# The order of the second half's turning and of its sums, and the last row tile's scaling, in a one-core decoder layer

## The chip, the cores and the metric

The kernel runs on one core of a Trainium2 chip. The metric is the device time of one execution in microseconds (us); of the kernel before there are three runs.

## What is computed

One decoder layer on x (1024 rows by 1024 channels): a layer norm, one input projection of the result h to 11,296 columns, two mixers on its parts (a gated short convolution and a chunked state-space scan), their output projections, a merge, a last projection and a layer norm of the residual. Cut to what matters here:

```
h = layer_norm(x, ln_in_g, ln_in_b)
proj = h @ w_in[i]
u, b_gate, c_gate, z_a, z_s, xbc, dt_raw, g_a, g_s = jnp.split(proj, offsets, axis=-1)
...
out = mixed @ w_o[i]
h = layer_norm(DEEPNORM_ALPHA * h + out, ln_g[i], ln_b[i])
```

## The kernel before

The input projection takes its weights' column tiles in 44 pairs of 128 + 128 columns. Each pair is multiplied with h by the seven products of a fast (Strassen-Winograd) 2x2 scheme. On the weights' side a pair has the blocks a11, a12, a21, a22 and four sums made of them: s1 = a21 + a22, s2 = s1 - a11, s3 = a11 - a21 (`combine`, L232) and s4 = a12 - s2 (`combine_last`, L248). On the side of h the four quarters (b11 and b21 from rows 0 to 511, b12 and b22 from rows 512 to 1023, each 512 of the 1024 channels) give four sums t1 = b12 - b11, t2 = b22 - t1, t3 = b22 - b12 and t4 = b21 - t2 (`quarter_sums`). Product 1 uses b11, 2 b21, 3 s4 with b22, 4 t4, 5 s1 with t1, 6 s2 with t2, 7 s3 with t3.

Every operand is split in two: a high part, a copy in TensorE's single-pass float32 format, and a low part, the remainder (`sub_split`, L104, shown as L105). A product of 128x128 weights with 512 columns is then three matmuls: high x high, high x low, low x high. The four k tiles of 128 channels make 12 matmuls for one product of one pair. The high part of a weight block is named whi, its low part wlo; there are four buffers of the one and three of the other. ACT makes the high parts of weights (L288; L286 for the chained ones of the first three pairs), DVE the low ones. The bank of a product is named p with product and pair (p3_0), or pU for products 1, 6 and 7. A t or b tile of one k with both its parts is a unit (`unit`).

The first three pairs run product by product, in the order 1, 2, 3, 6, 5, 7, 4 (pair 0, 1, 2 in each), since the quarters of the second half come later. Before, once products 1 and 2 are made, `dt_project(0)` makes a projection of 32 columns (the bank dps, copied by ACT to dT; a second half of it, `dt_project(1)`, and the transposes of dT follow among the matmuls of product 5), and `second_half` (L441) turns the rows 512 to 1023 by transposes on TensorE into eight banks, k = 4 to 7 (giving b22) and then 0 to 3 (giving b12). ACT scales each bank into hf (L394) and, for b22, DVE makes the unit: a cast (L398) and a remainder (L105). Product 3 needs b22, products 6, 5, 7 and 4 the sums.

The order on each engine comes from a scheduler that places instructions when their operands are expected, except where the code chains them: `q(engine, ...)` puts an instruction behind the last one that went through `q` on that engine. From the fourth pair on, `pin` keeps every engine in the order in which the code is written. Within an engine instructions run in their order. Before, the sums for the weights of the first three pairs are made on POOL through `q`, the first of the late ones held back until the layer norm's last scaling on DVE (`normed`); the operations of `quarter_sums` are left to the scheduler, k by k.

At the end the rows go out in eight tiles. `norm_out` (L1162) takes the mean and variance of a tile, ACT scales it (L1176), POOL multiplies and adds (L1177, L1178), SP sends it. For the last tile DVE does the first 832 columns alone (L1172, L1173) and ACT's queue sends those; the other 192 go the usual way.

## Time and profile before

| | |
|---|---|
| median of three runs (lowest, highest) | 1408.17 us (1406.65, 1409.61) |
| the profiled execution's own time | 1411.06 us |
| span from its first to its last instruction | 1408.9 us |
| mean granted TensorE clock | 0.992 |
| busy: PE, DVE, ACT, POOL | 1378.9, 975.2, 701.7, 485.3 us |

The engines are PE (TensorE), DVE (VectorE), ACT (ScalarE) and POOL (GpSimd); SP only issues transfers. A row of the order of time gives the start, the duration of one or of a merged run (xN), the engine, the line of the kernel's code, the operation, the output and inputs by tile name, and in brackets the idle time ahead of it and what ended that. Buffer numbers are left out of names, so `t<-t` stands for a t unit made from one of the sums. The granted clock is TensorE's clock as a share of its full one. PE's matmuls overlap: each row lasts 0.39 us, where the next starts earlier.

### The profile page before, as it was taken

The page shows a single profiled execution, that of the slowest core. Times are in us where ns is not written, and L with a number is a line of the kernel's source. Part 1 is how long each engine was busy: PE and PEld are TensorE (multiplying, and loading weights), DVE is VectorE, ACT ScalarE, POOL GpSimd, SP SyncE. Part 2 cuts the span into 40 slices and gives each one's busy share as a digit, 9 for nine tenths or more (in the row PEclk, how much of TensorE's full clock was granted, in tenths as well). Part 3 has the DMA queues.
Part 4 walks back from the last instruction along what each step waited for, and adds up shares of the span by engine and source line. Part 5 has one row for each costly group of instructions (what it writes and reads, how often), then busy time and mean ns, then how long its engine had stood idle before and what let it go on. Part 6 is the DMA issues. An engine that isn't in the chain of part 4 may idle for free.

```text
span 1408.9 us, 18441 instructions
## 1 busy us (share of the span) xinstructions
PE 1378.9 (98%) x6532; PEld 1110.0 (79%) x6532; DVE 975.2 (69%) x1422; ACT 701.7 (50%) x1228; POOL 485.3 (34%) x367
## 2 busy tenths in 40 slices
PE   8799999999999999999999999999999999999997
PEld 5577887888888888888888888888878888888886
DVE  8867779787779878688878686867464463224766
ACT  4565565656567555566566565555452231113431
POOL 1312215453435444334444343444230000000487
PEclk9899999999999999999999999999999999999999
DMA  6022363564454555544555445543457763223422
GB/s 239 16 76 94 115 145 110 129 180 129 141 134 133 153 155 147 131 131 130 151 157 187 132 154 127 153 128 127 172 174 269 232 222 139 100 75 110 144 90 90
DMA packets 166459, 198.09 MB, mean 141 GB/s; under 512 B 10688, under 2 KB 116064, under 8 KB 166368
## 3 DMA queue, kind: packets, MB, share of 16 engines
q1 hardware_dynamic: 158160, 167.14, 40.9%
q10 hardware_dynamic: 8208, 29.79, 5.3%
q8 instruction: 51, 0.84, 0.2%
q14 instruction: 40, 0.33, 0.1%
HBM read 146.28 MB, written 50.61 MB: 140 GB/s over the span
## 4 chain that ended last, share of the span: by engine, by line
PE 91%; DVE 4%; issue 2%; ACT 1%; POOL 1%; DMA 0%; ACTq 0%; POOLq 0%; DVEq 0%
PE p L1020 11%; PE p L1021 11%; PE p L1022 11%; PE pU L1020 8%; PE pU L1022 8%; PE pU L1021 8%; PE p_ws L859 4%; PE p_ws L860 4%; PE p_ws L861 4%; PE ya L691 2%; PE st L696 2%; PE p_wa L859 2%; PE p_wa L860 2%; PE p_wa L861 2%; PE p_wo L1157 2%
## 5 line engine op out<-in xcount | busy, mean ns | idle before, releaser
L105 DVE TENSOR_TENSOR wlop<-raw_a,whip 128x512 fp32r<-128x512 f32 x210 | 185.0, 881 | 160.5 <-ACT whip L288 64.7
L1020 PE MATMUL p<-b,whip 128*128 128x512 f32 x352 | 143.8, 409 | 7.6 <-ACT whip L286 4.8
L1020 PE MATMUL pU<-t,whip 128*128 128x512 f32 x352 | 145.2, 414 | 0.0
L1020 PE MATMUL p<-t,whip 128*128 128x512 f32 x352 | 142.0, 403 | 0.0
L1021 PE MATMUL p<-b,whip 128*128 128x512 f32 x352 | 140.4, 399 | 0.0
L1022 PE MATMUL p<-b,wlop 128*128 128x512 f32 x352 | 139.8, 398 | 0.0
L1021 PE MATMUL pU<-t,whip 128*128 128x512 f32 x352 | 139.3, 396 | 0.0
L1022 PE MATMUL p<-t,wlop 128*128 128x512 f32 x352 | 139.1, 395 | 0.0
L1021 PE MATMUL p<-t,whip 128*128 128x512 f32 x352 | 139.1, 395 | 0.0
L1022 PE MATMUL pU<-t,wlop 128*128 128x512 f32 x352 | 139.0, 395 | 0.0
L676 POOL TENSOR_TENSOR xw<-xd,dte_t 128x256 f32<-128x256 f32 x56 | 46.9, 837 | 260.5 <-DVE xd L662 260.5
L288 ACT ACTIVATE whip<-raw_a 128x512 fp32r<-128x512 f32 x207 | 125.8, 622 | 19.2 <-issue 10.5
L942 POOL TENSOR_TENSOR res<-res,ag 128x1024 f32<-128x1024 f32 x8 | 19.7, 2464 | 276.1 <-ACT res L941 276.1
L239 POOL TENSOR_TENSOR s<-raw_a,raw_a 128x512 f32<-128x512 f32 x42 | 69.6, 1657 | 92.1 <-DVE wlop L105 87.8
L860 PE MATMUL p_ws<-y,whis 128*128 128x512 f32 x256 | 100.9, 394 | 0.0
L859 PE MATMUL p_ws<-y,whis 128*128 128x512 f32 x256 | 100.8, 394 | 0.0
L861 PE MATMUL p_ws<-y,wlos 128*128 128x512 f32 x256 | 100.7, 393 | 0.0
L105 DVE TENSOR_TENSOR wlos<-raw_s,whis 128x512 fp32r<-128x512 f32 x32 | 22.1, 692 | 113.0 <-PE p_ws L861 89.2
L253 POOL TENSOR_TENSOR raw_a<-raw_a,s 128x512 f32<-128x512 f32 x42 | 67.5, 1606 | 90.2 <-issue 78.7
L105 DVE TENSOR_TENSOR wlop<-s,whip 128x512 fp32r<-128x512 f32 x84 | 80.2, 966 | 13.2 <-PE p L1022 8.5
L1020 PEld LDWEIGHTS p<-b,whip 128*128 128x128 f32 x352 | 67.0, 190 | 23.7 <-ACT whip L286 5.1
L288 ACT ACTIVATE whis<-raw_s 128x512 fp32r<-128x512 f32 x32 | 20.3, 634 | 129.6 <-PE p_ws L860 109.0
(225 smaller groups left out, 3404.7 us busy)
## 6 DMA issues: line engine op xcount, KB each, us to landing
raw_a<-in_w_in_dram SPq DMA_DIRECT2D x168, 256.0 KB, 4.0
em<-cum_d SPq DMA_DIRECT2D x64, 256.0 KB, 6.8
xg_d<-cv ACTq DMA_DIRECT2D x16, 512.0 KB, 7.0
xT<-xg_d SPq DMA_DIRECT2D x32, 256.0 KB, 4.7
z<-zs_d SPq DMA_DIRECT2D x32, 256.0 KB, 3.1
gat_d<-y SPq DMA_DIRECT2D x32, 256.0 KB, 2.8
gt<-gat_d SPq DMA_DIRECT2D x16, 512.0 KB, 6.4
raw_s<-in_w_s_dram SPq DMA_DIRECT2D x32, 256.0 KB, 4.3
```

The costliest lines, as they stand in the source:

```text
L105: return eng.tensor_tensor(lo, full, hi.bitcast(F32), ALU.subtract)
L239: fs = [lambda: Gp.tensor_tensor(s1, r["a21"], r["a22"], ALU.add), lambda: Gp.tensor_tensor(s2, s1, r["a11"], ALU.subtract), lambda: Gp.te ...
L253: f = lambda: Gp.tensor_tensor(a12, a12, s1s[p]["s2"], ALU.subtract)
L288: S.activation(flat(hi), src, AF.Copy)
L676: Gp.tensor_tensor(xw, XD[n, i], dte_t[:, hs, c].unsqueeze(2).to_broadcast([P, HG, HD]), ALU.mult)
L691: PE.matmul(YA[n][o:o + HD, t * P:(t + 1) * P], lhsT=XD[n, i][:, h, :], rhs=EM[n, i][:, h, :], start=True, stop=True)
L859: PE.matmul(ps, lhsT=hi[:, k, :], rhs=u[:, 0, :], start=start, stop=False)
L860: PE.matmul(ps, lhsT=hi[:, k, :], rhs=u[:, 1, :], start=False, stop=False)
L861: PE.matmul(ps, lhsT=lo[:, k, :], rhs=u[:, 0, :], start=False, stop=stop)
L1020: PE.matmul(ps, lhsT=hi[:, k, :], rhs=u[:, 0, :], start=first, stop=False, skip_group_check=True)
L1021: PE.matmul(ps, lhsT=hi[:, k, :], rhs=u[:, 1, :], start=False, stop=False, skip_group_check=True)
L1022: PE.matmul(ps, lhsT=lo[:, k, :], rhs=u[:, 0, :], start=False, stop=(k == 3), skip_group_check=True)
```

## The change

`second_half` becomes two parts. `lower_quarter` turns the banks k = 4 to 7 right after products 1 and 2, all 16 transposes, through `q`, ahead of the four evacuations. `upper_quarter` turns k = 0 to 3 after product 3 of pair 0. The sums of pair 1, and the last sum of pair 0, move from POOL to DVE. Pair 2's sums stay on POOL and wait until DVE has made the last b22 unit (`b22_done`). `quarter_sums` now makes all four tiles of t2, then t1, t3 and t4, with its sums, copies and remainders chained by `q`, some of them in place of b11. The units lie in other buffers (`PLACE`). The matmuls of products 3 and 6 of the first three pairs are chained as well. In `norm_out` ACT's scaling stands ahead of DVE's two operations and of the transfer on its queue, and DVE takes 704 columns of the last tile, ACT and POOL 320.

```diff
     B = {}
-    PLACE = {"t2": 0, "t1": 1, "t3": 2, "t4": 3}
+    PLACE = {"t2": range(4), "t1": range(4, 8), "t3": range(9, 16, 2), "t4": range(8, 16, 2)}
     def b_unit(n, k):
-        i = 4 * k + PLACE[n] if n in PLACE else 16 + 4 * ("b11", "b21", "b22").index(n) + k
+        i = PLACE[n][k] if n in PLACE else 16 + 4 * ("b11", "b21", "b22").index(n) + k
         B[n, k] = unit(i, f"{n}_{k}")
         return B[n, k]
...
         r = raws["p", p]
         s1, s2 = (est.tile([P, HALF], F32, name=f"e{n}_{p}") if p < 2 and n == "s1" else
                   r["a11"] if p < 2 else ap.tile([P, HALF], F32, tag=n, name=f"{n}_{p}") for n in ("s1", "s2"))
-        fs = [lambda: Gp.tensor_tensor(s1, r["a21"], r["a22"], ALU.add),
-              lambda: Gp.tensor_tensor(s2, s1, r["a11"], ALU.subtract),
-              lambda: Gp.tensor_tensor(r["a21"], r["a11"], r["a21"], ALU.subtract)]
+        eng = V if p == 1 else Gp
+        fs = [lambda: eng.tensor_tensor(s1, r["a21"], r["a22"], ALU.add),
+              lambda: eng.tensor_tensor(s2, s1, r["a11"], ALU.subtract),
+              lambda: eng.tensor_tensor(r["a21"], r["a11"], r["a21"], ALU.subtract)]
         if p < 2:
             fs = [fs[0], fs[2], fs[1]]
-        for f in fs:
-            q(Gp, f) if p < EARLY else f()
+        for i, f in enumerate(fs):
+            ins = q(eng, f) if p < EARLY else f()
+            if p == 2 and i == 0:
+                tc.add_manual_dep(ins.ins, b22_done[0].name,
+                                  mybir.DependencyInfo(mybir.DependencyClass.Sync, mybir.DependencyReason.DATA), reason="later")
         s1s[p] = {"s1": s1, "s3": r["a21"], "s2": s2}
     def combine_last(p):
...
         if "s4" in s1s[p]:
             return
         a12 = raws["p", p]["a12"]
-        f = lambda: Gp.tensor_tensor(a12, a12, s1s[p]["s2"], ALU.subtract)
-        if p < EARLY:
-            ins = q(Gp, f)
-            if p == 0:
-                tc.add_manual_dep(ins.ins, normed[0].name,
-                                  mybir.DependencyInfo(mybir.DependencyClass.Sync, mybir.DependencyReason.DATA), reason="later")
-        else:
-            f()
+        eng = V if p < 2 else Gp
+        f = lambda: eng.tensor_tensor(a12, a12, s1s[p]["s2"], ALU.subtract)
+        q(eng, f) if p < EARLY else f()
         s1s[p]["s4"] = a12
     def source(n):
...
     stats(7, 1)
     factors(6)
     norm(7, V)
-    normed = [last[V].ins]
     norm(6, S)
-    def second_half():
-        order = (4, 5, 6, 7, 0, 1, 2, 3)
-        trs = {k: bank(("c4", "tr", "st")[i % 3], f"tr1{k}") for i, k in enumerate(order)}
-        for k in order:
+    b22_done = []
+    def second_half(ks, tags):
+        trs = {k: bank(t, f"tr1{k}") for k, t in zip(ks, tags)}
+        for k in ks:
             for s in (4, 5, 7, 6):
-                PE.transpose(trs[k][:, s % 4 * P:(s % 4 + 1) * P], xs[s][:, k * P:(k + 1) * P], ident)
+                q(PE, lambda: PE.transpose(trs[k][:, s % 4 * P:(s % 4 + 1) * P], xs[s][:, k * P:(k + 1) * P], ident))
+        for k in ks:
             evac(1, k, trs[k])
-            if k in (5, 7, 1):
-                prep_hi(2 * EARLY + (5, 7, 1).index(k))
+    def lower_quarter():
+        combine_last(0)
+        prep_hi(2 * EARLY)
+        combine(1)
+        q(V, lambda: prep_lo(2 * EARLY))
+        second_half((4, 5, 6, 7), ("c4", "tr", "st", "cx"))
+        b22_done.append(last[V].ins)
+        combine_last(1)
+        prep_hi(2 * EARLY + 1)
+        q(V, lambda: prep_lo(2 * EARLY + 1))
+    def upper_quarter():
+        second_half((0, 1, 2, 3), ("cx", "st", "cx", "st"))
+        prep_hi(2 * EARLY + 2)
     def quarter_sums():
+        b11, b21, b12, b22 = ([hf[i][k][:, j * HALF:(j + 1) * HALF] for k in range(4)] for i in range(2) for j in range(2))
+        tt = [cv(f"t2_{i}") for i in range(2)]
+        t2 = [tt[k // 2][:, k % 2 * HALF:(k % 2 + 1) * HALF] for k in range(4)]
+        def split(n, k, src):
+            u = b_unit(n, k)
+            q(S, lambda: S.activation(u[:, 0, :], src, AF.Copy))
+            q(V, lambda: sub_split(u[:, 1, :], src, u[:, 0, :], V))
         for k in range(4):
-            b11, b21 = hf[0][k][:, :HALF], hf[0][k][:, HALF:]
-            b12, b22 = hf[1][k][:, :HALF], hf[1][k][:, HALF:]
-            tt = cv(f"t12_{k}"), cv(f"t34_{k}")
-            t = {"t1": tt[0][:, :HALF], "t2": tt[0][:, HALF:], "t3": tt[1][:, :HALF], "t4": tt[1][:, HALF:]}
-            V.tensor_tensor(t["t1"], b12, b11, ALU.subtract)
-            V.tensor_tensor(t["t2"], b22, t["t1"], ALU.subtract)
-            V.tensor_tensor(t["t3"], b22, b12, ALU.subtract)
-            V.tensor_tensor(t["t4"], b21, t["t2"], ALU.subtract)
-            for n in ("t2", "t1", "t3", "t4"):
-                u = b_unit(n, k)
-                S.activation(u[:, 0, :], t[n], AF.Copy)
-                sub_split(u[:, 1, :], t[n], u[:, 0, :], V)
+            q(V, lambda: V.tensor_tensor(b11[k], b12[k], b11[k], ALU.subtract))
+            q(V, lambda: V.tensor_tensor(t2[k], b22[k], b11[k], ALU.subtract))
+            split("t2", k, t2[k])
+        for k in range(4):
+            split("t1", k, b11[k])
+        for k in range(4):
+            q(V, lambda: V.tensor_tensor(b11[k], b22[k], b12[k], ALU.subtract))
+            split("t3", k, b11[k])
+        for k in range(4):
+            q(V, lambda: V.tensor_tensor(t2[k], b21[k], t2[k], ALU.subtract))
+            split("t4", k, t2[k])
...
         for k in range(4):
             first = k == 0 and (early and j in (1, 2, 3, 4, 5) or j in (1, 2, 5, 4))
             u = B[bn, k]
-            PE.matmul(ps, lhsT=hi[:, k, :], rhs=u[:, 0, :], start=first, stop=False, skip_group_check=True)
-            PE.matmul(ps, lhsT=hi[:, k, :], rhs=u[:, 1, :], start=False, stop=False, skip_group_check=True)
-            PE.matmul(ps, lhsT=lo[:, k, :], rhs=u[:, 0, :], start=False, stop=(k == 3), skip_group_check=True)
+            for w, v, stop in ((hi, 0, False), (hi, 1, False), (lo, 0, k == 3)):
+                f = lambda: PE.matmul(ps, lhsT=w[:, k, :], rhs=u[:, v, :], start=first and w is hi and v == 0, stop=stop,
+                                      skip_group_check=True)
+                q(PE, f) if 2 * EARLY <= now[0] < 3 * EARLY else f()
         oa, ob = O[p]
         oal, oah = oa[:, :HALF], oa[:, HALF:]
         if ob is not None:
...
         if n >= START and n - 2 in first_of:
             combine_last(first_of[n - 2])
         if n < START:
-            for k in range(n, min(n + LA + 1, 2 * EARLY if n < 2 * EARLY else START + LA)):
+            for k in range(n, min(n + LA + 1, 2 * EARLY if n < 2 * EARLY else 2 * EARLY + 2 if n == 2 * EARLY else START + LA)):
                 prep_hi(k)
                 if k < n + LA:
                     prep_lo(k)
...
             item_p(i, j, hi, lo)
             if n == 2 * EARLY - 1:
                 dt_project(0)
-                second_half()
+                lower_quarter()
+            if n == 2 * EARLY:
+                upper_quarter()
             if n == 3 * EARLY - 1:
                 quarter_sums()
             if n == 4 * EARLY + 1:
...
         r = res[s]
         mv = cst.tile([P, 2], F32, tag="mv", name=f"mv{s}", bufs=2)
         rs, nb = (cst.tile([P, 1], F32, tag="w" + n_, name=f"{n_}{s}", bufs=2) for n_ in ("rs", "nb"))
-        finish_stats(cst, st[s][:, :n, :], mv, rs, nb, "lo")
-        cut = 832 if last_row else 0
+        cut = 704 if last_row else 0
+        sl = slice(cut, D)
+        V.bn_aggr(mv, st[s][:, :n, :])
+        rsqrt(cst, rs, mv[:, 1:2], 1, "lo")
+        V.scalar_tensor_tensor(nb, mv[:, 0:1], -1.0, rs, ALU.mult, ALU.mult)
+        S.activation(r[:, sl], r[:, sl], AF.Identity, bias=nb, scale=rs)
         if last_row:
             V.scalar_tensor_tensor(r[:, :cut], r[:, :cut], mv[:, 0:1], lg[:, :cut], ALU.subtract, ALU.mult)
             V.scalar_tensor_tensor(r[:, :cut], r[:, :cut], rs, lb[:, :cut], ALU.mult, ALU.add)
             S.dma_start(out[s * P:(s + 1) * P, :cut], r[:, :cut])
-        sl = slice(cut, D)
-        S.activation(r[:, sl], r[:, sl], AF.Identity, bias=nb, scale=rs)
         Gp.tensor_tensor(r[:, sl], r[:, sl], lg[:, sl], ALU.mult)
         Gp.tensor_tensor(r[:, sl], r[:, sl], lb[:, sl], ALU.add)
         SP.dma_start(out[s * P:(s + 1) * P, sl], r[:, sl])
```

What the built programs hold at three places follows; numbers of tiles are kept where the set has to be seen (t3_2 is quarter k = 2 of t3, whip0_5 the high part of pair 0's weights for product 5).

On DVE, behind the last scaling of the layer norm, stood the first units of b22:

```order
L383 TENSOR_SCALAR x7_174<-x7_174,rs_t_119,nb_t_120 128x1024
L398 CAST b22_0_499<-hf10_497 128x512
L105 TENSOR_TENSOR b22_0_499<-hf10_497,b22_0_499 128x512
L398 CAST b22_1_508<-hf11_506 128x512
L105 TENSOR_TENSOR wlop0_3_567<-e0_a12_161,whip0_3_512 128x512
```

and now

```order
L376 TENSOR_SCALAR x7_174<-x7_174,rs_t_119,nb_t_120 128x1024
L252 TENSOR_TENSOR e0_a12_161<-e0_a12_161,e0_a11_150 128x512
L234 TENSOR_TENSOR es1_1_488<-e1_a21_176,e1_a22_178 128x512
L236 TENSOR_TENSOR e1_a21_176<-e1_a11_157,e1_a21_176 128x512
L235 TENSOR_TENSOR e1_a11_157<-es1_1_488,e1_a11_157 128x512
L99 TENSOR_TENSOR wlop0_3_492<-e0_a12_161,whip0_3_486 128x512
L391 CAST b22_0_516<-hf10_514 128x512
```

Four sums that POOL made, and a weight remainder, have come ahead of the first cast of b22.

On ACT, the copies that make the high parts, around the weights of product 5 (whip0_5); before:

```order
L463 ACTIVATE t2_1_649<-t12_1_643 128x512
L1045 ACTIVATE oa2_409<-p3_2_611 128x512
L463 ACTIVATE t3_1_655<-t34_1_644 128x512
L463 ACTIVATE t4_1_658<-t34_1_644 128x512
L286 ACTIVATE whip0_5_699<-es1_0_246 128x512
L463 ACTIVATE t1_2_670<-t12_2_661 128x512
L463 ACTIVATE t3_2_673<-t34_2_662 128x512
```

and now

```order
L468 ACTIVATE t3_3_672<-hf03_301 128x512
L468 ACTIVATE t4_0_676<-t2_0_625 128x512
L468 ACTIVATE t4_1_680<-t2_0_625 128x512
L468 ACTIVATE t4_2_684<-t2_1_626 128x512
L468 ACTIVATE t4_3_688<-t2_1_626 128x512
L279 ACTIVATE whip0_5_693<-es1_0_246 128x512
L279 ACTIVATE whip1_5_710<-es1_1_488 128x512
```

The copy of product 5's weights stood between the second and third quarter's copies; now it follows the last copy of t4.

On DVE, the sums and remainders of the t units; before, in the third quarter:

```order
L457 TENSOR_TENSOR t12_2_661<-hf12_518,hf02_296 128x512
L459 TENSOR_TENSOR t34_2_662<-hf12_518 128x512
L458 TENSOR_TENSOR t12_2_661<-hf12_518,t12_2_661 128x512
L105 TENSOR_TENSOR t1_2_670<-t12_2_661,t1_2_670 128x512
L460 TENSOR_TENSOR t34_2_662<-hf02_296,t12_2_661 128x512
L105 TENSOR_TENSOR t2_2_667<-t12_2_661,t2_2_667 128x512
L105 TENSOR_TENSOR t3_2_673<-t34_2_662,t3_2_673 128x512
L105 TENSOR_TENSOR t4_2_676<-t34_2_662,t4_2_676 128x512
```

and now, in the last quarter of t3 and in t4:

```order
L478 TENSOR_TENSOR hf03_301<-hf13_529 128x512
L99 TENSOR_TENSOR t3_3_672<-hf03_301,t3_3_672 128x512
L481 TENSOR_TENSOR t2_0_625<-hf00_286,t2_0_625 128x512
L99 TENSOR_TENSOR t4_0_676<-t2_0_625,t4_0_676 128x512
L481 TENSOR_TENSOR t2_0_625<-hf01_291,t2_0_625 128x512
L99 TENSOR_TENSOR t4_1_680<-t2_0_625,t4_1_680 128x512
L481 TENSOR_TENSOR t2_1_626<-hf02_296,t2_1_626 128x512
L99 TENSOR_TENSOR t4_2_684<-t2_1_626,t4_2_684 128x512
L481 TENSOR_TENSOR t2_1_626<-hf03_301,t2_1_626 128x512
L99 TENSOR_TENSOR t4_3_688<-t2_1_626,t4_3_688 128x512
L99 TENSOR_TENSOR wlop0_5_708<-es1_0_246,whip0_5_693 128x512
```

Sums of several sets stood between a sum and its remainder; now each remainder follows its own sum, and product 5's weight remainder follows all of them.

6 lines of the change are left out of this document (1 added, 5 removed).

## The prediction

> **What bounds the kernel now.** I read the page's engine table first, then what PE waited for in the first 180 us, then the granted clock in stretches of 2 us, and last the order of time on each engine. (In a row of PE waits: total us, times, longest; in a row of stretches: PE's busy us, its matmuls, the granted clock.)
>
> ```profile
> PE 1378.9 (98%) x6532; PEld 1110.0 (79%) x6532; DVE 975.2 (69%) x1422; ACT 701.7 (50%) x1228; POOL 485.3 (34%) x367
> ...
> PE p L1020 <- ACT whip L286: 4.8, 1, 4.8
> PE tr L446 <- ACT hf L394: 2.9, 3, 1.7
> ...
> PE dps L476 <- DVE t L105: 0.6, 1, 0.6
> ...
> 20.00:22.00 2.00, 1.57 (x4) 0.57 1.05 386
> 22.00:24.00 2.00, 2.00 (x7) 0.57 0.95 315
> ...
> 50.00:52.00 2.00, 0.29 (x3) 0.75 0.00 0
> ...
> 56.00:58.00 2.00, 2.00 (x6) 0.50 0.00 0
> ...
> 60.00:62.00 2.00, 2.00 (x8) 0.69 0.00 0
> 62.00:64.00 2.00, 2.00 (x10) 1.00 0.00 0
> ```
>
> PE is busy 98% of the span, so only a stretch in which it is idle or slowed can give or take time. The change touches one: the turning of the second half and the products behind it. There PE waits 4.8 us for the high part of weights, 2.9 us for banks and twice 0.6 us for t units, and then runs at clock 0.50. Now that stretch on PE:
>
> ```profile
> 42.07 0.39 PE L476 MATMUL dps<-b,wdt 128*64 128x512 f32 x1
> ...
> 55.12 0.80 PE L1020 MATMUL p<-b,whip 128*128 128x512 f32 x1 [4.82 <-ACT whip L286]
> ...
> 69.89 0.40 PE L1021 MATMUL p<-t,whip 128*128 128x512 f32 x1
> ...
> 81.38 0.39 PE L1022 MATMUL p<-t,wlop 128*128 128x512 f32 x1
> ...
> 86.51 0.40 PE L476 MATMUL dps<-b,wdt 128*64 128x512 f32 x1
> ...
> 91.65 0.40 PE L1020 MATMUL pU<-t,whip 128*128 128x512 f32 x1
> ```
>
> Product 3 starts at 55.12. The first two matmuls of product 5 of pair 0 are done by 69.89; the third, at 81.38, starts the rest of product 5, among it five dps matmuls from 86.51. At 91.65 product 7 begins. So 81.38 to 91.65, 10.27 us, held 34 matmuls of product 5, five of dps and the turning of dT, without a wait. From there on every engine's listed order is the same before and after the change until the last row tile. PE has no idle time left to absorb a shift, so I cost the first part as the shift of 91.65.
>
> **The front of the stage: what it removes.** The other engines there:
>
> ```profile
> 22.42 0.42 DVE L398 CAST b<-hf 128x512 fp32r<-128x512 f32 x1
> ...
> 23.48 0.42 DVE L398 CAST b<-hf 128x512 fp32r<-128x512 f32 x1
> ...
> 40.36 0.81 DVE L383 TENSOR_SCALAR x<-x,rs_t,nb_t 128x1024 f32<-128x1024 f32 x1
> 44.70 0.75 DVE L398 CAST b<-hf 128x512 fp32r<-128x512 f32 x1 [3.53 <-ACT hf L394]
> 45.48 1.65 DVE L105 TENSOR_TENSOR b<-hf,b 128x512 fp32r<-128x512 f32 x1
> ...
> 55.81 0.68 DVE L105 TENSOR_TENSOR b<-hf,b 128x512 fp32r<-128x512 f32 x1
> ...
> 62.07 1.89 DVE L105 TENSOR_TENSOR t<-t,t 128x512 fp32r<-128x512 f32 x3
> ...
> 41.30 1.29 POOL L253 TENSOR_TENSOR e_a<-e_a,e_a 128x512 f32<-128x512 f32 x1 [21.48 <-issue]
> ...
> 52.96 1.44 POOL L253 TENSOR_TENSOR raw_a<-raw_a,s 128x512 f32<-128x512 f32 x1
> ...
> 42.55 0.59 ACT L477 ACTIVATE dT<-dps 64x512 f32<-64x512 f32 x1 [0.95 <-PE dps L476]
> ```
>
> Three remainders in 1.89 us: a DVE operation with two SBUF inputs takes 0.60 us when they follow each other, and a split (cast and remainder) 1.06 us (22.42 to 23.48). While POOL works through its nine sums (41.30 to 54.40), the same remainder takes 1.65 us: DVE and POOL take turns, one POOL sum (about 1.1) before each DVE operation. So the split of b22 ended only at 56.49. In the changed kernel DVE makes pair 0's last sum and pair 1's three, 4 x 0.60, and a weight remainder in 41.2 to 44.4. That lies inside the 3.53 us in which DVE waited for its first bank, so it costs nothing; without that cover it would be 3.0 us. PE must now take bank c4 first and waits for the copy of dT (42.55 + 0.59), 0.7 us. The four splits then run from 44.75 to 49.0 instead of 56.49, and product 3 of pair 0 from about 45.7, paced by them. Nearly all of the old 4.8 + 2.9 us goes, and with it the slow clock of 55 to 61 us. If that were all, the change would be worth some 10 us.
>
> **Where the gain goes.** What PE needs next, the weights' high part for product 5, no longer stands among the copies of the t units on ACT but behind all of them:
>
> ```profile
> 68.13 0.63 ACT L286 ACTIVATE whip<-es 128x512 fp32r<-128x512 f32 x1
> ...
> 75.32 0.68 DVE L458 TENSOR_TENSOR t<-hf,t 128x512 f32<-128x512 f32 x1
> ...
> 76.04 0.63 ACT L463 ACTIVATE t<-t 128x512 fp32r<-128x512 f32 x1 [0.52 <-DVE t L458]
> ```
>
> At 68.13 stands the old copy, made while half of the t units were missing. In the changed order it follows the copy of t4's last quarter, which follows t4's last sum on DVE. And there each sum is followed at once by the remainder that needs ACT's copy of it: sum 0.68, 0.04 to the copy, copy 0.63, 0.03 back is 1.38 us from the sum's start (75.32 to 76.67), then the remainder 0.60, so 1.98 us a quarter where the work is 1.20. Before, other quarters' operations stood in these gaps.
>
> DVE's queue, added up from these rows: at 49.0 the splits are done. Pair 1's last sum, and a wait: PE ends product 3 of pair 0 0.5 after the last split, ACT copies its bank (0.6) and then pair 1's weights (0.63): 50.9 with the steps between. POOL's four sums of pair 2 now start at 49.0, so three DVE operations take 1.65 each: 55.9. POOL is done at 55.2; copy 0.63, three weight remainders and t2's first remainder: 59.0. t2's other quarters, two sums that hang together, copy, remainder, 2.6 each: 66.9. t1's remainders, 4 x 0.60: 69.3. t3: a first quarter of 2.4 with two bank additions in its gap, then 3 x 1.98: 77.6. t4: 3 x 1.98 gives 83.6, the last sum 0.72, its copy and the weights' copy 0.53 + 0.63: 85.5. I add 0.5 for steps between dependent operations and take **86.0**. PE has by then long done products 3 and 6 and dps, eight matmuls of which come after t1's last remainder (69.3): about 72.4. So it waits some 14 us in one piece, before product 5 of pair 0. Bounds of the 86.0: 80.5 if the gaps of t3 and t4 (7 x 0.78) were hidden, 88 if every turn with POOL and every round trip takes 0.2 more.
>
> From 86.0: 36 matmuls instead of 34 and no dps, three matmuls fewer at 10.27/39, about 0.25 each: 9.5 us at full clock. PE comes out of such a wait at half clock. By the stretches, 0.69 over 60:62 is half clock for 1.2 us of it, so the wait before 55.12 cost 6.1 us at half clock; 0.57 twice, over 20:24, is 3.4 us after a smaller wait. Half the clock loses half of that, 3.0 or 1.7 us. The wait ahead is longer than either, and I take 2.5. Product 7 then begins at 86.0 + 9.5 + 2.5 = 98.0, against 91.65: **+6.35 us**.
>
> The Trainium skill, "TensorE: Matmul & The Clock Gate", section "What's actually happening", lets one busy window of about 3.4 us end the slow state. This trace has it once as that and once nearly twice as long; by the rule alone the loss would be 1.7, an estimate, and the sum 0.8 lower.
>
> **The last row tile.**
>
> ```profile
> 1383.01 2.25 DVE L102 SCALAR_TENSOR_TENSOR nb<-mv,rs 128x1 f32<-128x1 f32 x1
> ...
> 1396.36 2.40 POOL L1177 TENSOR_TENSOR res<-res,lg 128x1024 f32<-128x1024 f32 x1 [1.43 <-ACT res L1176]
> ...
> 1401.59 0.16 DVE L102 SCALAR_TENSOR_TENSOR nb<-mv,rs 128x1 f32<-128x1 f32 x1
> ...
> 1402.77 1.08 DVE L1173 SCALAR_TENSOR_TENSOR res<-res,rs,lb 128x832 f32<-128x832 f32 x1
> ...
> 1395.04 1.24 ACT L1176 ACTIVATE res<-res,nb,rs 128x1024 f32<-128x1024 f32 x1 [4.85 <-DVE nb L102]
> ...
> 1403.95 0.37 ACTq L1174 DMA_DIRECT2D out_dram<-res  x1
> 1404.36 0.55 ACT L1176 ACTIVATE res<-res,nb,rs 128x192 f32<-128x192 f32 x1 [3.46 <-DVE res L1173]
> 1404.99 0.59 POOL L1177 TENSOR_TENSOR res<-res,lg 128x192 f32<-128x192 f32 x1 [3.79 <-ACT res L1176]
> 1405.65 0.59 POOL L1178 TENSOR_TENSOR res<-res,lb 128x192 f32<-128x192 f32 x1
> ...
> out_dram<-res ACTq DMA_DIRECT2D x1, 416.0 KB, 2.4
> out_dram<-res SPq DMA_DIRECT2D x1, 96.0 KB, 1.7
> ```
>
> Today ACT's scaling stands behind the output transfer that waits for DVE, and POOL ends at 1406.24. In the changed order ACT starts at 1401.8: 320 columns by the slope from 192 (0.55) to 1024 (1.24) are 0.66, so 1402.5. POOL takes 0.87 for 320 columns by its two rows, twice. DVE's two operations shrink to 704/832 of 1.08 = 0.92. They now run beside POOL, and a DVE operation of that form beside POOL took 2.25 instead of 0.16, so again turns: 1402.6 DVE, 1403.4 POOL, 1404.3 DVE, 1405.1 POOL. That is 1.1 us earlier, with a transfer of 160 KB, between 1.7 and 2.4, say 1.85: -0.95 us. Without turns -1.9; at worst, with both transfers meeting, -0.5.
>
> **Sum.** +6.35 - 0.95 = +5.4. The profiled execution took 1411.06 (span 1408.9 and 2.2 around it), 2.9 above the median of the runs; its own time would become 1416.5, and the median 1408.17 + 5.4 = **1413.6**. By the bounds (86.0 by -1 to +1.5 from the additions, clock 1.7 to 3.0, tail -1.9 to -0.5) this case spans 1410.8 to 1416.0.
>
> **Rivals.** About 0.2%, 2.8 us, is what the measurement of this kernel tells from no change.
>
> *The round trips are hidden* (0.11). If DVE does not stand still between a sum and its remainder in t3 and t4, the weights come at 80.5: 80.5 + 9.5 + 2.5 is 0.9 after 91.65, and with the tail it is 1408.1, no change. For it: the DVE row at 62.07 shows remainders back to back. Against: those had finished copies; here the copy's sum stands directly ahead in the same queue.
>
> *The weights' copy overtakes* (0.07), the faster case. If ACT makes product 5's copies before those of t3 and t4, as at 68.13 today, and DVE their remainders, PE goes on at 72: 72.4 + 9.5 - 91.65 = -9.7, with the tail 1397.5. It decides from the point where that copy starts before about 79. For it: that is all that is missing, since t1 is ready at 69.3. Against: ACT's rows of the trace stand in the listed order, none before its turn.
> The same page of the skill (its table) calls ACT and DVE strict queues; by that this rival has no chance, and I leave it a small one for an error in my reading of the order.
>
> *The wait is repaid twice* (0.09). The weights' buffers (four high, three low) run dry during the wait, so products 5 and 7 also wait for each next copy behind ACT's other work: three more waits of up to 1 us, 1416.6, and up to 1418 with the longer clock. Against: ACT needs 0.63 a copy and PE 12 x 0.25 an item.
>
> The forecast keeps 0.73, of which 0.02 lie within 0.2%. So slower 0.71 + 0.09 = 0.80, same 0.11 + 0.02 = 0.13, faster 0.07. The range for 8 in 10 is 1409.5 to 1417.5: it leaves out the faster case, most of the no-change case and the far end of the double one.
>
> **What would show it.** In PE's waits after: one wait of 12 to 15 us before a product 5 matmul, released by ACT's weights' copy, where the 4.8 and most of the 2.9 are gone; the granted clock 0.50 during and behind it; product 3 of pair 0 before 50 us. On DVE, splits of b22 at 1.06 us, and t3 and t4 with idle gaps of about 0.8 released by ACT. On POOL, four sums from 49. At the end ACT's scaling directly behind nb, and POOL done about 1.1 us sooner behind the last statistics. The forecast is wrong if product 5 starts before 82 us, if the wait stands elsewhere, or if the clock comes back at once.

## The result, and the profile after

The changed kernel takes 1416.56 us, the median of four executions (1415.91 to 1417.25); the kernel before, beside it, 1408.08. The ratio is 1.0052 (95% interval 1.004 to 1.0065): slower, by half a per cent. (A ratio is not simply that of the two medians beside it, which here would be 1.0060.) With five more executions of the changed kernel beside 23 of the kernel before it was 1.0053 (1.004 to 1.0067). The forecast was 1413.6, in a range of 1409.5 to 1417.5. All figures here and below leave out three executions at a far lower granted clock: 2261.36 and 2392.53 us of the kernel before and 1935.11 of one version below.

One thing in the description of the change has to be put right: of the early products only product 3's matmuls are chained, product 6's are not. The weights' high copies from product 3 on are chained on ACT in both kernels; what is new is that the copies of the t units go through the same chain.

PE's waits in the first 180 us of the changed kernel (total us, times, longest), its order of time where the wait ends, and the granted clock in stretches of 2 us (PE's busy us, then the other engines', the clock third from the end):

```profile
PE p L1039 <- ACT whip L279: 14.5, 2, 14.0
```

```profile
72.49 0.39 PE L494 MATMUL dps<-b,wdt 128*64 128x512 f32 x1
86.89 1.22 PE L1039 MATMUL p<-t,whip 128*128 128x512 f32 x2 [14.01 <-ACT whip L279]
...
98.36 0.63 PE L1039 MATMUL pU<-t,whip 128*128 128x512 f32 x2
```

```profile
76.00:78.00 2.00, 0.00 (x0) 0.00 (x0) 1.29 (x2) 0.58 (x2) 0.00 (x0) 0.99 0.00 0
78.00:80.00 2.00, 0.00 (x0) 0.00 (x0) 1.29 (x2) 0.58 (x2) 0.00 (x0) 0.50 0.00 0
...
88.00:90.00 2.00, 2.00 (x6) 1.57 (x5) 0.85 (x2) 0.40 (x1) 1.06 (x1) 0.50 0.00 0
90.00:92.00 2.00, 2.00 (x7) 1.58 (x6) 0.00 (x0) 0.10 (x1) 1.92 (x3) 0.60 0.00 0
92.00:94.00 2.00, 2.00 (x10) 1.63 (x9) 1.29 (x2) 1.67 (x3) 0.81 (x1) 1.00 0.00 0
```

The waits of 4.8 and 2.9 us before product 3 are gone but for 0.7 us behind the copy of dT, and in their place stands one of 14.0 before product 5, released by ACT's copy of its weights. The clock drops during it and is back near 91.6. Product 7 begins at 98.36, 6.7 us behind the 91.65 of before. In the same profiles the first matmul of pair 3 stands at 115.16 instead of 108.45, again 6.7: nothing between product 7 and there takes the shift up.

Now DVE, POOL and ACT in the changed kernel:

```profile
44.41 0.43 DVE L391 CAST b<-hf 128x512 fp32r<-128x512 f32 x1 [0.27 <-ACT hf L387]
...
48.06 0.69 DVE L99 TENSOR_TENSOR b<-hf,b 128x512 fp32r<-128x512 f32 x1
...
52.32 1.78 DVE L472 TENSOR_TENSOR hf<-hf,hf 128x512 f32<-128x512 f32 x1
...
82.86 0.69 DVE L481 TENSOR_TENSOR t<-hf,t 128x512 f32<-128x512 f32 x1
84.31 0.69 DVE L99 TENSOR_TENSOR t<-t,t 128x512 fp32r<-128x512 f32 x1 [0.76 <-ACT t L468]
84.91 0.69 DVE L481 TENSOR_TENSOR t<-hf,t 128x512 f32<-128x512 f32 x1
86.36 0.69 DVE L99 TENSOR_TENSOR t<-t,t 128x512 fp32r<-128x512 f32 x1 [0.76 <-ACT t L468]
```

```profile
48.83 1.66 POOL L234 TENSOR_TENSOR s<-raw_a,raw_a 128x512 f32<-128x512 f32 x1 [29.26 <-DVE b L99]
```

```profile
85.69 0.63 ACT L468 ACTIVATE t<-t 128x512 fp32r<-128x512 f32 x1 [1.42 <-DVE t L481]
86.23 1.14 ACT L279 ACTIVATE whip<-es 128x512 fp32r<-128x512 f32 x2
```

Four splits run from 44.41 to 48.7, POOL's late sums start behind them, DVE's operations beside those take 1.7 to 1.8, and then each quarter of t3 and t4 is a sum, 0.76 us of nothing while ACT copies, and the remainder: 2.05 us a quarter (82.86 to 84.91). ACT's copy of product 5's weights follows directly on the copy of t4's last quarter.

The last row tile, the order of time and then the transfer from its issue (KB, us to landing):

```profile
1408.28 0.16 DVE L1193 SCALAR_TENSOR_TENSOR nb<-mv,rs 128x1 f32<-128x1 f32 x1
...
1408.53 0.65 ACT L1194 ACTIVATE res<-res,nb,rs 128x320 f32<-128x320 f32 x1 [0.93 <-DVE nb L1193]
...
1409.33 1.53 DVE L1197 SCALAR_TENSOR_TENSOR res<-res,rs,lb 128x704 f32<-128x704 f32 x1
1410.20 1.39 POOL L1200 TENSOR_TENSOR res<-res,lb 128x320 f32<-128x320 f32 x1
```

```profile
out_dram<-res SPq DMA_DIRECT2D x1, 160.0 KB, 2.1
```

POOL ends 3.31 us behind the start of nb, before 4.65. The last transfer takes 2.1 instead of 1.7, and the span ends 6.7 behind nb instead of 7.3.

### The profile page after: what moved, and what is told of

It reads as the page before. It is cut to its first block, busy times and chain, and to the rows that moved or that the text cites. A ratio compares the mean times of both kernels' runs of the same rounds, so it can differ in the third digit from the quotient of the medians.

```text
span 1415.0 us, 18439 instructions
## 1 busy us (share of the span) xinstructions
PE 1378.8 (97%) x6532; PEld 1110.6 (78%) x6532; DVE 977.4 (69%) x1427; ACT 702.0 (50%) x1228; POOL 479.5 (34%) x362
## 4 chain that ended last, share of the span: by engine, by line
PE 92%; DVE 4%; ACT 1%; issue 1%; DMA 1%; POOL 0%; SPq 0%; POOLq 0%; ACTq 0%; DVEq 0%
PE p L1039 33%; PE pU L1039 25%; PE p_ws L877 4%; PE p_ws L878 4%; PE p_ws L879 4%; PE ya L709 2%; PE st L714 2%; PE p_wa L877 2%; PE p_wa L878 2%; PE p_wa L879 2%; PE p_wo L1179 2%; PE p_wo L1178 2%; PE p_wo L1177 2%; PE yb L704 2%; PE tr L668 1%
## 5 line engine op out<-in xcount | busy, mean ns | idle before, releaser
L1039 PE MATMUL p<-t,whip 128*128 128x512 f32 x704 | 226.2, 402 | 14.0 <-ACT whip L279 14.0
L1039 PE MATMUL p<-b,whip 128*128 128x512 f32 x704 | 226.2, 402 | 3.7 <-DVE ob L1048 2.7
L1039 PE MATMUL pU<-t,whip 128*128 128x512 f32 x704 | 228.1, 405 | 0.3 <-ACT t L468 0.3
L1039 PEld LDWEIGHTS p<-t,whip 128*128 128x128 f32 x704 | 131.1, 190 | 43.6 <-ACT whip L279 14.5
L1039 PEld LDWEIGHTS pU<-t,whip 128*128 128x128 f32 x704 | 132.1, 189 | 32.5 <-ACT t L468 1.1
L1039 PEld LDWEIGHTS p<-b,whip 128*128 128x128 f32 x704 | 129.7, 189 | 35.2 <-ACT a L836 2.5
L1039 PE MATMUL pU<-b,whip 128*128 128x512 f32 x352 | 114.6, 407 | 2.5 <-DVE b L391 1.9
L660 ACT ACTIVATE em<-em,cum_t 128x128 f32<-128x128 f32 x256 | 81.3, 390 | 6.9 <-ACT ob L604 3.6
```

The costliest lines, as they stand in the source:

```text
L660: S.activation(em[:, h, :], em[:, h, :], AF.Relu, bias=cum_t[:, 8 * g + 4 * i + h, c:c + 1], scale=-1.0)
L1039: f = lambda: PE.matmul(ps, lhsT=w[:, k, :], rhs=u[:, v, :], start=first and w is hi and v == 0, stop=stop, skip_group_check=True)
```

## The experiments

The theory is that of the forecast: PE stands still because the copies of product 5's weights wait on ACT behind t3 and t4, whose quarters each hold a round trip between DVE and ACT, and it comes out of the wait at half clock. The rival is that the sums set by set, DVE's extra sums or POOL's turns with DVE cost by themselves, wherever the weights stand. Two more questions were what half clock costs, and why the medians differ by more than the profiles. I give product 7's first matmul as a measure of the stage, since the time as a whole also moves for other reasons (the last experiments).

The profiles differ ahead of the stage already. In ten of them the granted clock is at a half for some 3.4 us near 22 us, and the last dps matmul before the turning stands at 41.8 to 42.6 us; in the other four (product 5's weights ahead, the sums k by k, both cures, the changed kernel once more) the clock is 1.00 there and it stands at 40.5 to 40.7. Where a version of the one group is compared with one of the other, some 1.3 us go with that and not with the edit.

**Product 5's weights ahead of t3 and t4.**

```diff
             split("t1", k, b11[k])
+        yield
         for k in range(4):
             q(V, lambda: V.tensor_tensor(b11[k], b22[k], b12[k], ALU.subtract))
...
             if n == 3 * EARLY - 1:
-                quarter_sums()
+                sets = quarter_sums()
+                next(sets)
+            if n == 4 * EARLY - 1:
+                next(sets, None)
```

> The changed kernel, but t3's and t4's sums, copies and remainders are recorded behind product 6, so that the copies and remainders of product 5's weights stand ahead of them on ACT and DVE. t3 and t4 still stand ahead of product 7's weights. Theory A (the place of the weights' copies behind t3 and t4 is what holds PE): the 14.0 us wait before product 5 is gone (under 1 us) and one of 11 to 13 us stands before product 7 instead; product 7 begins at 93 to 95 us instead of 98.4, in half clock, and the time falls by 2 to 4, to 1412.5 to 1414.5. Rival B (the sums set by set keep PE waiting by their amount, wherever the weights stand): the wait before product 5 stays above 10 us and the time at 1416 to 1417.

1413.71 us, ratio 1.004 (1.0024 to 1.0056). Its waits and PE's order of time:

```profile
PE pU L1040 <- ACT whip L279: 12.0, 1, 12.0
```

```profile
93.42 1.22 PE L1040 MATMUL pU<-t,whip 128*128 128x512 f32 x2 [12.02 <-ACT whip L279]
```

The wait has left product 5 and stands before product 7, whose weights are still behind t4. So it goes where the weights' copies go, as expected, and the rival falls for this wait. Of the 4.9 us by which product 7 begins sooner than in the changed kernel, 1.1 lie ahead of the stage.

**Each set directly behind the weights needed sooner.** As above, with a second `yield` ahead of t4:

```diff
+            if n in (3 * EARLY - 1, 4 * EARLY - 1, 5 * EARLY - 1):
+                next(sets, None)
```

> The changed kernel, with t3's sums, copies and remainders recorded behind product 6 and t4's behind product 5, so that each set comes ahead of the product that needs it and behind the weights needed sooner. The same work, nothing left out. Theory A: no wait above 5 us is left behind product 3; some 3 us before product 7 and 1 us before product 4 remain, the clock is down for at most 3.5 us, product 7 begins at 84 to 86 us instead of 98.4, and the time falls by 8 to 11 to 1405.5 to 1408.5, about the kernel before. Rival B (set by set costs by itself: round trips of 0.76 us a quarter, DVE's turns with POOL): the waits move but their sum stays above 10 us, 1413 to 1417.

1408.14 us, ratio 0.9992 (0.9983 to 1.0001).

```profile
85.70 1.22 PE L1041 MATMUL pU<-t,whip 128*128 128x512 f32 x2 [3.17 <-ACT whip L279]
...
97.79 1.25 PE L1041 MATMUL p<-t,whip 128*128 128x512 f32 x4 [0.70 <-ACT whip L279]
```

```profile
86.00:88.00 2.00, 2.00 (x5) 1.41 (x5) 2.00 (x4) 1.97 (x3) 0.00 (x0) 0.50 0.00 0
...
90.00:92.00 2.00, 2.00 (x6) 1.54 (x6) 1.68 (x4) 0.68 (x2) 0.00 (x0) 0.57 0.81 319
```

The order of the sets against the weights is worth 8.4 us by the medians, the whole loss of the change. But a wait of 3.2 us is left, and the clock is down from about 84.9 to 91.7, twice as long as I expected. From 85.70 on that is 6.0 us at half clock, some 3 us lost beside the wait itself.

**The round trips.** In t3 and t4 each remainder is recorded one sum later; the weights stay where the change has them.

```diff
+        def pipelined(n, src, make, ks=range(4)):
+            us = {}
+            for k in ks:
+                q(V, lambda: make(k))
+                us[k] = b_unit(n, k)
+                q(S, lambda: S.activation(us[k][:, 0, :], src[k], AF.Copy))
+                if k:
+                    q(V, lambda: sub_split(us[k - 1][:, 1, :], src[k - 1], us[k - 1][:, 0, :], V))
+            q(V, lambda: sub_split(us[3][:, 1, :], src[3], us[3][:, 0, :], V))
...
-            split("t4", k, t2[k])
+        pipelined("t4", t2, lambda k: V.tensor_tensor(t2[k], b21[k], t2[k], ALU.subtract))
```

> The changed kernel with each remainder of t3 and t4 recorded one sum later, so that DVE makes the next sum while ACT copies. Nothing else moves: product 5's weights still stand behind t4. Theory A (seven or eight idle gaps of 0.76 us on DVE are part of the wait): the gaps go, product 5's wait falls from 14.0 to 8 to 9.5 us, product 7 begins 5 to 6 earlier, at 92.5 to 93.5, and the time is 1410.5 to 1412. Rival E (the gaps cost nothing, DVE's rate is set elsewhere, for example by remainders that now stand beside other work and take longer): the wait stays above 12 us and the time above 1415.

1409.37 us, ratio 1.0003 (0.9992 to 1.0014). DVE, then PE:

```profile
78.64 0.69 DVE L488 TENSOR_TENSOR t<-hf,t 128x512 f32<-128x512 f32 x1
79.24 0.69 DVE L99 TENSOR_TENSOR t<-t,t 128x512 fp32r<-128x512 f32 x1
79.84 0.69 DVE L488 TENSOR_TENSOR t<-hf,t 128x512 f32<-128x512 f32 x1
```

```profile
81.83 1.22 PE L1045 MATMUL p<-t,whip 128*128 128x512 f32 x2 [8.58 <-ACT whip L279]
```

A quarter takes 1.20 us instead of 2.05, and product 5's wait falls from 14.0 to 8.6: 5.4 of the 14 were round trips. Product 7 begins at 92.95, as expected. The time is 1.1 us below what I expected. The profiled execution, 1411.19, lies 5.6 below that of the changed kernel, which is what the stage shows; the median lies 7.2 below, and the executions spread from 1407.95 to 1412.70 with granted clocks from 0.995 to 0.991.

**Both cures.** t3 behind product 6, t4 behind product 5, remainders one sum later.

> Both cures together: t3 recorded behind product 6, t4 behind product 5, and in each a remainder one sum later. The run with t3 and t4 late and not pipelined gave 1408.1 and kept a wait of 3.2 us before product 7, which cost 7 us at half clock. Theory A: that wait falls below 1 us, the clock stays at 1.00 from 45 to 110 us, product 7 begins at 81 to 82.5 us, and the time is 1402 to 1405, below the kernel before. Rival F (the time lost moves on to the next weights, those of product 4, and a wait of 3 us or more with half clock stands there): 1406 to 1408.5.

1400.21 us (1398.85 to 1400.61), ratio 0.9929 (0.9916 to 0.9941): it beats the kernel before by 0.7% and, by the medians, the changed one by 1.2%. That is more than I expected. PE's order of time and two stretches of 10 us:

```profile
79.99 0.63 PE L1047 MATMUL pU<-t,whip 128*128 128x512 f32 x2
```

```profile
64.00:74.00 10.00, 10.00 (x45) 7.54 (x44) 9.27 (x17) 5.51 (x10) 0.48 (x1) 1.00 0.00 0
74.00:84.00 10.00, 10.00 (x49) 7.34 (x48) 10.00 (x15) 8.35 (x13) 6.94 (x3) 1.00 0.00 0
```

PE does not stand still in these 20 us and the clock stays at 1.00; product 7 begins 11.7 us before that of the kernel before, 1.4 of it from ahead of the stage; the other 10.2 are the "some 10 us" at which the prediction put the front of the stage. What separates this version from the one with late sets is the wait of 3.2 us and the 0.7 before product 4; the removal of these, with the half clock behind the first, was worth 7.9 us by the medians. Product 7 comes 5.7 sooner and pair 3's first matmul 9.0 (97.63 for 106.64); 1.2 of each come from ahead of the stage, and the 7.8 left at pair 3 agree with the medians. A new wait of 1.6 us, for a bank addition on DVE, stands in pair 3 at 118.96.

**The sums k by k again**, with the early lower quarter, the sums on DVE and the new last row tile kept; the units go back to their old buffers.

```diff
-        for k in range(4):
-            q(V, lambda: V.tensor_tensor(b11[k], b12[k], b11[k], ALU.subtract))
-            q(V, lambda: V.tensor_tensor(t2[k], b22[k], b11[k], ALU.subtract))
-            split("t2", k, t2[k])
...
+            for n in ("t2", "t1", "t3", "t4"):
+                u = b_unit(n, k)
+                S.activation(u[:, 0, :], t[n], AF.Copy)
+                sub_split(u[:, 1, :], t[n], u[:, 0, :], V)
```

> The changed kernel with the sums of the t units made k by k and not chained, as before; the early lower quarter, the second pair's sums on DVE and the new last row tile stay. Theory A (only the set-by-set order, with the weights behind it, costs): no wait above 2 us behind product 3, no half clock there, and a time of 1403.5 to 1407, 9.5 to 13 below the changed kernel. Rival B (the moved quarter, the sums on DVE and POOL's turns with DVE cost by themselves): waits of 5 us or more stay between 45 and 80 us and the time is 1411 to 1416.

1407.62 us, ratio 0.9986 (0.9976 to 0.9995).

```profile
55.35 0.73 PE L1029 MATMUL p<-b,whip 128*128 128x512 f32 x2 [1.13 <-ACT whip L279]
56.94 0.79 PE L1029 MATMUL p<-b,wlop 128*128 128x512 f32 x1 [0.86 <-DVE wlop L99]
...
71.68 0.44 PE L483 MATMUL dps<-t,wdt 128*64 128x512 f32 x1 [1.28 <-ACT t L471]
```

The long wait is gone with the set-by-set order, so the other parts of the change do not cost the time. The gain is smaller than expected: short waits of 0.5 to 1.3 us remain at 55 to 57 and 67 to 73, and the clock is at 0.50 behind both groups (58 to 60, 74 to 76), which I had excluded.

**The early quarter taken away instead.** The kernel before with only the quarter sums of the best version.

```diff
-    PLACE = {"t2": 0, "t1": 1, "t3": 2, "t4": 3}
+    PLACE = {"t2": range(4), "t1": range(4, 8), "t3": range(9, 16, 2), "t4": range(8, 16, 2)}
...
-                quarter_sums()
+                sets = quarter_sums()
+            if n in (3 * EARLY - 1, 4 * EARLY - 1, 5 * EARLY - 1):
+                next(sets, None)
```

> The kernel before, its second half turned as before and its last row tile as before, with only the quarter sums of the version that gave 1400.2 (t2 and t1 set by set, t3 behind product 6, t4 behind product 5, remainders one sum later). Theory A (the early lower quarter and the order of the sums only pay together): the 4.8 and 2.9 us before product 3 and the half clock stay, nothing waits behind them, and the time is 1407.5 to 1409.5, no change. Rival J (the order of the sums is the whole gain of that version): 1400 to 1403.

1408.86 us, ratio 1.0002 (0.9992 to 1.0011). The wait before product 3 is the old one:

```profile
55.10 0.79 PE L1038 MATMUL p<-b,whip 128*128 128x512 f32 x1 [4.82 <-ACT whip L286]
```

Product 7 begins 2.7 us sooner than in the kernel before (88.99), but a new wait of 1.3 us for a bank addition on DVE, at 127.67, gives part of that back. So neither the early quarter (with the rest of the change) and sums k by k (0.9986) nor the new sums with the old front (1.0002) brings much; together they bring 0.7%.

**The pair sums back on POOL**, in the best version: the last sum of pair 0 and the four of pair 1, held back until the layer norm's last scaling on DVE as in the kernel before.

```diff
-        eng = V if p == 1 else Gp
+        eng = Gp
...
-        eng = V if p < 2 else Gp
+        eng = Gp
```

> The version that gave 1400.2, with the sums of pair 0 (its last) and pair 1 back on POOL, held back until the last tile is normalized as before. Theory A (those four operations are free on DVE, and on POOL they take turns with b22's splits): the first splits of b22 take about 1.65 us an operation instead of 0.43 and 0.69, product 3 begins 2 to 4 later and stands still between its matmuls, product 7 begins 3 to 6 later and the time is 1403 to 1406. Rival I (POOL makes them for nothing there): 1399.5 to 1401.

1403.43 us, ratio 0.9965 (0.9954 to 0.9976), 3.2 above the version with these sums on DVE. DVE, then POOL:

```profile
46.38 1.65 DVE L99 TENSOR_TENSOR b<-hf,b 128x512 fp32r<-128x512 f32 x1
47.95 1.50 DVE L394 CAST b<-hf 128x512 fp32r<-128x512 f32 x1
49.48 0.69 DVE L99 TENSOR_TENSOR b<-hf,b 128x512 fp32r<-128x512 f32 x1
```

```profile
46.14 1.34 POOL L235 TENSOR_TENSOR e_a<-es,e_a 128x512 f32<-128x512 f32 x1
47.55 1.60 POOL L252 TENSOR_TENSOR e_a<-e_a,e_a 128x512 f32<-128x512 f32 x1
```

While POOL is at work, the first remainder takes 1.65 us and the second cast 1.50; once it is done, a remainder takes 0.69. Product 7 begins at 85.11 instead of 79.99; 2.0 of that lie ahead of the stage, and the 3.1 left agree with the medians. So the price of these sums on POOL is real. On DVE they cost nothing, as the prediction had it: in the changed kernel DVE still waits 0.27 us for its first bank behind them (the row at 44.41).

**What half clock costs behind the 14 us wait.** Matmuls without use keep PE busy in it.

```diff
+    def fill():
+        fps = bank("st", "fill")
+        ins = dps_last[0]
+        for i in range(52):
+            with tc.issue_after(ins.ins):
+                ins = PE.matmul(fps[:2 * H, :], lhsT=wdt[:, 0, :], rhs=B["b11", 0][:, 0, :], start=True, stop=True)
```

> The changed kernel with 52 more matmuls of the dps shape on PE, into a bank that nothing reads, between the last dps matmul and the 14 us wait: added work without use that keeps PE busy for 12 of the 14 us, so that only the clock differs. Theory A (the wait itself costs the time, and half clock behind it 2.3 us more): the wait shrinks to about 2 us, product 5 still begins at 86.9, the granted clock is 1.00 behind it, product 7 begins at 96.0 instead of 98.4, and the time is 1413.8 to 1414.8. Rival D (the slow clock is most of the loss, here and further on): 1411 or less.

1415.52 us, ratio 1.0041 (1.0028 to 1.0053); the profiled execution took 1414.32.

```profile
73.19 12.26 PE L493 MATMUL fill<-b,wdt 128*64 128x512 f32 x52
87.39 1.26 PE L1048 MATMUL p<-t,whip 128*128 128x512 f32 x4 [1.94 <-ACT whip L279]
...
96.79 0.40 PE L1048 MATMUL pU<-t,whip 128*128 128x512 f32 x1
```

```profile
88.00:90.00 2.00, 2.00 (x10) 1.63 (x10) 1.35 (x3) 0.90 (x2) 0.57 (x1) 1.00 0.00 0
```

At full clock product 5 takes 9.40 us (87.39 to 96.79), in the changed kernel 11.47 (86.89 to 98.36): half clock costs 2.07. By the medians, from two sets of runs, it is 1.0, with intervals that meet, and the time is 0.7 above what I expected. Product 5 begins 0.5 later than in the changed kernel because all of this profile stands 0.5 later ahead of the stage. The wait itself is the loss and the clock the smaller part.

**The last row tile alone**, in the kernel before: `norm_out` as in the diff of the change.

> The kernel before with the last row tile of the change alone (ACT's scaling of 320 columns ahead of the first output transfer, cut at 704). Theory A: nothing moves ahead of the last row tile; ACT's scaling follows nb directly, POOL is done about 1.3 us sooner behind nb, the last transfer (160 instead of 96 KB) takes 0.4 more, and the time falls by 0.5 to 0.95, to 1407.2 to 1407.7. Rival C (the tail costs: both transfers end together and the larger one is last): +0.3 to +0.8.

1407.80 us, ratio 0.9996 (0.9986 to 1.0005): no change that can be told. In its profile the span ends 6.4 us behind nb instead of 7.3. That is the size of the forecast's term, but the same code ended 6.7 behind nb in the changed kernel, and the time does not confirm it.

**The kernel before once more, and the changed kernel once more.**

> The kernel before, unchanged, profiled once more. Question: the first profile's execution took 1411.06 us, 2.9 above the median of the timed executions, and I carried the profiled difference over to the median. Theory A (that execution drew an unlucky phase of the PE clock around 55 us, 6.1 us at half clock): another profiled execution shows the same waits (4.8 before product 3, 2.9 for the banks), a half clock of 3.4 to 4.7 us, and an own time of 1407 to 1409.5. Rival (a profiled execution always takes about 2.9 more than a timed one): 1411 again, with the same rows.

> The changed kernel, unchanged, beside more runs of the kernel before. Theory A (the forecast's +5.4 holds for two executions with the same slow stretches of the clock; the profile of before happened to have all of them): the difference of the medians is 7 to 8.5, the changed kernel at 1415.5 to 1417, and a second profile shows 13.5 to 14.5 us before product 5. Rival H (the median of before in the first runs was low by chance): 5 to 6.5.

The kernel before: profiled at 1410.62 us, with the same waits and half clock from 51 to 61 again, so my theory missed. But the rival does not hold either: the profiled executions of other versions lie on both sides of their medians (1398.89 and 1400.21 with both cures, 1415.40 and 1415.81 for the changed kernel, 1411.19 and 1409.37 without the round trips). The timed executions of the kernel before reach from 1406.5 to 1411.3, with a mean granted clock of 0.995 at the lower end and 0.992 at the upper; 0.003 of 1409 us is 4.2 us, nearly all of that spread. Both of its profiles are from the upper end. The changed kernel: 1415.81, 7.4 above the kernel before (1408.40), as theory A had it; its second profile has a wait of 14.0 too, and its nine executions lie within 1415.4 to 1417.3, all at 0.990 or 0.991.

**The wait before product 3 in the kernel before, filled.** (`ins` is the last transpose of the second half.)

```diff
+        fps = bank("cx", "fill")
+        for i in range(18):
+            with tc.issue_after(ins.ins):
+                ins = PE.matmul(fps[:2 * H, :], lhsT=wdt[:, 0, :], rhs=B["b11", 0][:, 0, :], start=True, stop=True)
```

> The kernel before with 18 more matmuls of the dps shape, into a bank that nothing reads, on PE behind the last transpose of the second half: added work without use that fills about 4.2 of the 4.8 us before product 3. Question: what the half clock of 51 to 61 us cost the kernel before, and whether its spread comes from there. Theory A (the granted clock differs from one execution to the next, and what it costs at 55 us is carried on to product 7): the clock is 1.00 from 50 to 62 us, product 7 begins 1.5 to 3 earlier than the 91.65 of the first profile, and the median is 1406 to 1407.5. Rival G (PE then runs into t2's units, which DVE makes no sooner, and waits for these instead): new waits of 1.5 to 3.5 us in all before product 6's matmuls, product 7 at 90.8 to 91.7, and 1408 to 1409.5.

1410.52 us (1408.92 to 1411.45), ratio 1.0011 (1.0002 to 1.0019): no gain, rather a loss.

```profile
55.84 0.50 PE L1024 MATMUL p<-b,whip 128*128 128x512 f32 x1 [1.42 <-ACT hf L394]
66.84 0.50 PE L1025 MATMUL pU<-t,whip 128*128 128x512 f32 x1 [1.25 <-DVE t L105]
70.52 0.96 PE L1024 MATMUL pU<-t,whip 128*128 128x512 f32 x3 [1.54 <-ACT t L467]
```

The clock is 1.00 through the stage, but product 3 starts 0.7 later (its first matmul now waits for ACT's last scaling of a bank, not for the weights), PE now waits for t2's units, and product 7 begins at 91.36, hardly sooner than the 91.65. This is rival G in its mechanism. That the median lies above G's range, and that no execution is below 1408.9, it does not explain; nor do the times of these eleven executions go with their granted clocks, as they do in the kernel before. This stays open.

## Why the prediction was right, and where it was not

- **The wait and its cause**: shown. One wait of 14.0 us before product 5 (forecast "some 14"), released by ACT's weights' copy. It moved with the weights and shrank with the round trips.
- **Product 5's start**: forecast 86.0, measured 86.89. The steps up to t1 came out closely: DVE's three operations beside POOL end at 55.95 (forecast 55.9), though no POOL sum takes the "about 1.1" (1.27 to 1.75 in the two kernels), and t1 ends at 69.68 (69.3). Then t3's second quarter takes 2.59 us, not 1.98, since ACT copies dT ahead of its copy, and the five quarters behind it 2.05 each. The 0.5 added for steps covers part of this.
- **Product 5's length**: 9.5 at full clock, measured 9.40. **The half clock**: 2.5 forecast, 2.07 measured; the 1.7 by one window of 3.4 us, which the prediction weighed beside it, was a little too low. The three together: product 7 at 98.0 forecast, 98.36 measured, +6.7 for +6.35.
- **The last row tile**: -0.95 forecast, -0.6 measured between nb and the end of the span. POOL gained 1.3 instead of 1.1, and the transfer took 2.1 instead of the assumed 1.85. It is too small to be told in the time.
- **The sum for the profiled execution**: 1416.5 forecast, 1416.76 measured. That it is so close is in part luck: product 5 started 0.9 late and the last row tile gained 0.35 less, while the half clock cost 0.4 less and 1.8 us instead of 2.2 stand around the span.
- **The step that failed** is the last one, "the median 1408.17 + 5.4 = **1413.6**". It took the profiled execution of before to lie 2.9 above the median for a reason that the changed kernel would share. It does not: the changed kernel's profile is 0.2 from its median. Of the 3.0 us by which the forecast fell short, 0.3 lie in the sum for the profiled execution and the rest here. What the 2.9 consist of can be read from the version with the last row tile alone, which up to that tile is the kernel before:

```profile
58.00:60.00 2.00, 2.00 (x9) 1.57 (x8) 2.00 (x4) 1.54 (x3) 0.00 (x0) 0.75 0.42 131
...
90.60 0.39 PE L1020 MATMUL pU<-t,whip 128*128 128x512 f32 x1
```

The wait before product 3 is the same (4.83 us), but half clock lasts 3.9 us behind it instead of 6.1, and product 7 begins 1.05 sooner than at the 91.65 of before. Behind a wait near 217 us it has no half clock, where before has 3.4 us of it, worth 1.7 (the last section). The two make 2.75. The half clock near 22 us, some 1.3, can be missing too, as in four of the 14 profiles. Both profiles of the kernel before have all three, the one behind product 3 at 5.9 and 6.1 us; its 63 timed executions go with the clock, from 1406.7 on average at 0.995 to 1410.3 at 0.992. The changed kernel has half clock behind its 14 us wait and near 224 us in both its profiles, and all its executions are at 0.990 or 0.991.
- **The range** held in part by luck. The bounds of the case itself end at 1416.0, below the measured 1416.56; the range reached further for the sake of the rival in which the wait is repaid twice, and that rival's 1416.6 is the number measured. Only the profile decides against it: from 86.89 to 180 us PE waits for no copy of weights again.
- **The rivals**: the gaps stood there (0.76 us each), so the round trips were not hidden. No copy overtook. The wait was not repaid twice.

## What to carry to other kernels

Making operands set by set is only as good as the place of the next product's other operand in the same queues: look where each copy of weights stands among the units on ACT, and put each set behind the weights that are needed sooner. Where one engine makes a sum, a second copies it and the first needs the copy back, record the step that needs it one sum later; here that took a quarter from 2.05 to 1.20 us. When a forecast is carried from a profile to a median, find out first which draws of the clock the profile holds; a wait of 3 us can cost twice its length.

## What the runs showed of the hardware

Half clock differs between executions in which everything else is alike. In the kernel before and in the version with the new last row tile alone, PE waits equally long near 217 us; the rows are PE's order of time and the stretch of 2 us behind the wait, first of before, then of the other:

```profile
217.88 1.73 PE L691 MATMUL ya<-em,xd 128*64 128x128 f32 x16 [2.24 <-DVE em L668]
```

```profile
218.00:220.00 2.00, 2.00 (x17) 1.48 (x18) 1.97 (x4) 0.00 (x0) 0.90 (x1) 0.57 0.69 273
```

```profile
216.81 1.26 PE L691 MATMUL ya<-em,xd 128*64 128x128 f32 x16 [2.23 <-DVE em L668]
```

```profile
218.00:220.00 2.00, 2.00 (x11) 1.71 (x10) 1.97 (x2) 0.83 (x3) 1.88 (x2) 1.00 0.40 110
```

PE waits 2.2 us there in all 14 profiles of this study; nine have a stretch of half clock behind this wait, and five have none; where it occurs it costs about 1.7 us (0.43 and 0.42 of two stretches of 2 us). The Trainium skill, "TensorE: Matmul & The Clock Gate", section "What's actually happening", says that the window in which activity is counted runs freely and does not start with the kernel. That agrees with draws of this kind. It does not say how the share of a window that is idle decides, and the runs here do not settle it: once PE was at work again, half clock lasted about 3.4 us here, 4.7 in the changed kernel behind the 14 us, 6.0 with late sets behind 3.2 us, and 6.1 in the kernel before behind 4.8 us, but 3.9 behind the same 4.8 us in the version with the last row tile alone. With the sums k by k it came behind groups of waits of which none was longer than 1.3 us.
